# Loads of mem in fewer, longer pieces, and the short convolution behind the other mixers

## The chip, the cores and the metric

The kernel runs on one core of one Trainium2 chip. The metric is the device time of one execution in microseconds (us), the median of several runs. Engines are named as in the profile: PE is TensorE (PEld its weight loads), DVE is VectorE, ACT is ScalarE, POOL is GpSimd, SP is SyncE, which here only issues DMAs.

## The reference

One layer of an encoder for 256 tokens of width 2048, all in float32, with 256 rows of memory for the cross attention:

```python
mem_n = rms_norm(mem, mem_norm_g)
h = rms_norm(x, norm_g[l, 0])
q, k, v, g, lr, u_f, u_h, u_s = jnp.split(h @ w_in[l], split_at, axis=-1)
y_a = gla_mixer(q, k, v, g, lr, ...)                      # gated linear attention
y_b = rms_norm(fnet_mixer(u_f), grp_norm_g[l, 0])         # Fourier mixer
y_c = rms_norm(hyena_mixer(u_h, hy_conv_w[l], filt, hy_skip[l]), grp_norm_g[l, 1])
y_d = rms_norm(shortconv_mixer(u_s, sc_conv_w[l]), grp_norm_g[l, 2])
mix = jnp.concatenate([y_a, y_b, y_c, y_d], axis=-1)
x = x + mix @ w_out[l]
x = x + cross_attention(rms_norm(x, norm_g[l, 1]), mem_n, w_xq[l], w_xkv[l], w_xo[l])
x = x + swiglu(rms_norm(x, norm_g[l, 2]), w_gate_up[l], w_down[l])
return rms_norm(x, final_norm_g)
```

The short convolution mixer is small: `b, c, h = split(u)`, then `b * short_conv(c * h)`, a convolution of three taps along the tokens. Each of the four mixers gives 512 of the 2048 columns of `mix`.

## The kernel before

**Precision and the weight stream.** Each float32 operand of a large product is split in two parts, high and low, and a product is three matmuls: high by high, high by low, low by high (`part_rows`, L345 to L347, for results with tokens on the partitions; `mm`, L296 and L297, for results with features on the partitions). The weights are laid out in HBM in the order of their use, in slabs of 128 x 2048. `Stream._half` loads a slab from SP (L81) into one of three `raw` buffers, and for each half of it (1024 columns) makes the high part on ACT (`wh`, L102) and the low part on DVE (`wl`, L103). `Stream.take` hands the blocks to the products and keeps three halves ahead in this part of the kernel. Activations that enter a product are split likewise into slots of 512 columns, `act[0]` to `act[23]` (act_76 to act_99 in the program): `split`, with the high part from ACT (L206) and the low part from DVE (L198).

**The start.** `w_xkv` comes first, on `mem`. The first slab is loaded in four pieces (256, 256, 512 and 1024 columns), the next ones in halves, as long as the list `st.after` is not empty. After each piece one entry of that list is called; an entry loads parts of `memT` into `res` (`load`, L413), one part being 128 rows of 1 KB (256 columns of float32). Part 0 comes separately (`mem0`). Ten entries load parts 1 to 15: parts 1 to 5 one by one, then pairs. `start_m(n)` scales and splits part n into slot n right before the n-th k-step of the product (L210 on ACT, L202 on DVE).

**The background.** While PE works through the long products, the mixers advance step by step as Python generators in `Background.q`. Behind each matmul group `poll` goes through the list from its front and advances each entry whose time has come, as long as the estimated debt of DVE (`owed`) is small. So an entry nearer to the front has its instructions emitted first when several are due. `drain(g)` advances one generator to its end. Each generator's instructions go into the in-order queues of PE, ACT and DVE between those of the weight stream; a scheduler in the framework then settles the final order on each engine.

**Around the change.** In `mixers`, the Fourier mixer (`fn.mix`) and the gated linear attention (`gl.mix`, GLA) are added at the end of the list; the short convolution (`short_conv`) is added later, at position 0, so ahead of them, and advanced by its first step at once (`go`), which issues the loads of its inputs from POOL. Its further steps are the three-tap convolutions (`conv3`), the products with the first third of `u` (which comes from the last `w_in` product, `ev_s`), and `group_norm`: squares, sums over features on PE (`rstd_begin`, L244), a reciprocal root in small DVE steps (`rstd_cols`, L255 to L258 and helpers), two diagonal matrices `dgh` and `dgl` (`rstd_end`, L273 on ACT and L202 on DVE), a pair of matmuls that spreads the scale over all partitions (L280), a copy of it to `rs` (L283), and the scaled and split result. GLA ends in the same kind of norm, one pair of L280 for each of its four heads; its scaled output is `go`, the gated product `gg`.

**`out_proj`.** The product with `w_out` follows. It takes its sixteen k-steps in four parts in this order: Hyena (slots 16 to 19), Fourier (0 to 3), GLA (4 to 7), short convolution (20 to 23). Ahead of the second, third and fourth part `ready` drains the mixer that the part needs, and then issues loads of rows of `x` into the `res` buffers that this mixer has given up (L714, and L413 for `xT`):

```python
self.mix = act[4:8] + act[0:4] + act[16:24]
return self.gemm_rows("w_out", [0, 512], self.mix, parts=[range(k, k + 4) for k in (8, 4, 0, 12)], before=ready)
```

with `before` being `lambda n: self.bg.drain((g_fn, g_gla, g_sc)[n])`. Each k-step has two column groups and two row groups, twelve matmuls. When the product is done, `add_rows` adds `x` to it.

Of the kernel before, what the change touches and what calls it, by code (L numbers as in the profile page):

```python
# [169 lines left out]
class Block:  # L170
# [219 lines left out]
    def run(self):  # L390
        nc, cp = self.nc, self.cp
        st = self.st
        self.act = [cp.tile([P, 512], F32R, name=f"act{i}") for i in range(24)]
        self.res = [cp.tile([P, 4, R], F32, name=f"res{i}") for i in range(4)]
        self.resk = lambda i: self.res[i // 4][:, i % 4, :]
        self.vec = cp.tile([P, NV], F32, name="vec")
        self.onesr = cp.tile([P, P], F32R, name="ones")
        self.ones = self.onesr.bitcast(F32)
        self.ident = cp.tile([P, P], F32, name="ident")

        self.sq = [cp.tile([P, 8], F32, name=f"sq{i}") for i in range(2)]
        self.mg = cp.tile([P, 16], F32, name="mg")
        self.eps = cp.tile([P, 8], F32, name="eps")[:, 0:1]
        self.gap(cp, 416)

        self.kd = self.outside("keys", KT)
        self.xf = [self.outside(n, KT) for n in ("features1", "features2")]
        self.qf = self.outside("queries", KT)
        self.sf, self.gf, self.gq = (self.outside(n, 4) for n in ("products", "gates", "gla"))
        self.ff = self.outside("hidden", FT)  # L410
        self.vd = nc.dram_tensor("values", (P, 8 * 512), F32, kind="Internal").ap()
        def load(src, k, n):
            nc.sync.dma_start(self.res[k // 4][:, k % 4:k % 4 + n, :].rearrange("p k r -> p (k r)"),  # L413
                              self.t[src][:, k * R:(k + n) * R])

        self.load_x = lambda k, n: load("xT", k, n)

        nc.vector.memset(self.ones, 1.0)

        p = self.bank()  # L420
        for _ in range(10):
            nc.tensor.matmul(p[:, 0:P], self.ones, self.ones, start=True, stop=True)
        nc.vector.memset(self.eps, EPS)
        nc.scalar.copy(self.eps, self.eps)
        st.after = [lambda: None, lambda: None]
        st.after += [lambda a=a: load("memT", *a) for a in ((1, 1), (2, 1), (3, 1), (4, 1), (5, 1), (6, 2), (8, 2), (10, 2), (12, 2), (14, 2))]
        st.after.append(lambda: nc.sync.dma_start(self.vec, self.t["vecs"]))
        make_identity(nc, self.ident)
        with self.tc.tile_pool(name="wx", bufs=1) as st.extra:
            self.attention(self.mixers())  # L430
        self.mlp()
# [5 lines left out]
    def mixers(self):  # L437
# [63 lines left out]
        def short_conv(u0):  # L501

            m = []
            for k in range(4):
                m.append(self.tmp())
                self.load_turned(m[-1], self.sf, k)
            yield FAR
            for j in range(4):
                m[j] = self.conv3(m[j], V_SCW + 3 * j)
                yield  # L510
            sq = []
            for j in range(4):
                while len(u0) <= j:
                    yield
                y = self.res[1][:, j, :]
                self.tt(y, y, m[j], ALU.mult)
                sq.append(self.tmp())
                nc.scalar.activation(sq[j], y, AF.Square)
                if j > 1:
                    self.tt(sq[j - 1], sq[j - 2], sq[j - 1], ALU.add)  # L520
                yield SOON
            yield from self.group_norm(self.res[1], 2, act[20:24], total=sq[2:])

        with tc.tile_pool(name="mid", bufs=1) as mid:
            self.dgp = mid
            gl = Gla(self, mid)
            with tc.tile_pool(name="hyp", bufs=1) as hyp, tc.tile_pool(name="k2", bufs=8) as k2:
                hy = Hyena(self, hyp, k2)

                mem0 = hy.piece()[:, 0:R + 16]  # L530
                nc.sync.dma_start(mem0, self.t["mem0"])
                self.bg.add(prepare(mid))

                for cols in ([0, 512], [1024], [1536]):
                    first = dict(parts=[[k] for k in range(KT)], before=start_m) if len(cols) > 1 else {}
                    for c, ps in zip(cols, self.gemm_rows("w_xkv", cols, h, **first)):
                        for r in range(2):
                            self.store_turned(self.kd, c // P, r, hy.piece(), ps[r][:, :])
                for hd in range(4):
                    for r, p in enumerate(self.gemm_rows("w_xkv", [D + hd * 512], h, start_x if hd == 3 else rows.append)[0]):  # L540
                        for c in range(2):
                            v, o = self.tmp(), (2 * hd + r) * 512 + c * R
                            nc.scalar.activation(v, p[:, c * R:(c + 1) * R], AF.Copy, scale=self.rcm[:, r:r + 1])
                            nc.gpsimd.dma_start(self.vd[:, o:o + R], v)
                    if hd < 2:
                        self.load_x(8 * hd, 4)
                        self.load_x(8 * hd + 4, 4)
                self.bg.drain()

                def ev_u(i, p):  # L550
                    hy.feed(i, self.merge(p))
                    if i == 4:
                        self.bg.add(hy.convs())

                self.gemm("w_in", [UH + i * P for i in range(12)], h, ev_u)
                for r, p in enumerate(self.gemm_rows("w_in", [512], h, lambda k: k or low_rank())[0]):
                    nc.scalar.copy(gl.v[r], p)
                for r, p in enumerate(self.gemm_rows("w_in", [0], h)[0]):
                    for j in range(0, 512, R):
                        self.store_turned(self.gq, j // P, r, self.tmp(), p[:, j:j + R])  # L560
                gl.fetch()
                fn = Fnet(self, act[20:24])
                fn.feed(self.gemm_rows("w_in", [UF], h)[0])
                self.bg.drain()

            with tc.tile_pool(name="glp", bufs=1) as glp:
                gl.open(glp)
                fn.open(glp)
                g_fn = self.bg.add(fn.mix(act[0:4], gl))
                g_gla = self.bg.add(gl.mix(act[4:8]))  # L570
                halves = [(r, j) for r in range(2) for j in range(0, 512, R)]
                ps = self.gemm_rows("w_in", [US + 512], h)[0]
                c = [self.tmp() for _ in halves]
                for t, (r, j) in zip(c, halves):
                    nc.scalar.copy(t, ps[r][:, j:j + R])
                ps = self.gemm_rows("w_in", [US + 1024], h)[0]
                for t, (r, j) in zip(c, halves):
                    self.tt(t, ps[r][:, j:j + R], t, ALU.mult)
                    self.store_turned(self.sf, j // P, r, self.tmp(), t)
                u0 = []  # L580
                g_sc = self.bg.add(short_conv(u0), 0, True)
                ps = self.gemm_rows("w_in", [1024], h)[0]
                for r, j in halves:
                    t = self.tmp()
                    nc.scalar.activation(t, ps[r][:, j:j + R], AF.Silu)
                    self.store_turned(self.gf, j // P, r, self.tmp(), t)
                for k in range(4):
                    self.load_turned(gl.gate[k], self.gf, k)

                def ev_s(i, p):  # L590
                    u0.append(i)
                    self.merge(p, self.res[1][:, i, :])

                self.gemm("w_in", [US + i * P for i in range(4)], h, ev_s)
                gl.done = True
                return self.out_proj(lambda n: self.bg.drain((g_fn, g_gla, g_sc)[n]))
# [429 lines left out]
class Hyena:  # L1026
# [100 lines left out]
    def load(self):  # L1127

        nc, t = self.b.nc, self.b.t
        nc.sync.dma_start(self.tab, t["dft"][:, 512:1024])  # L1130
        fwd = self.piece()
        nc.sync.dma_start(fwd, t["dft"][:, 0:512])
        small = self.piece()
        c33, w2 = small[0:33, 0:R + 64], small[0:64, R + 64:R + 128]
        nc.sync.dma_start(c33, t["c33"])
        nc.sync.dma_start(w2, t["c64"][0:64, 0:64])
        self.loaded = fwd, c33, w2
        self.decay(0)
# [508 lines left out]
```

## Time and profile before

| | us |
|---|---|
| median of 3 runs | 1478.79 (1477.31 to 1478.9) |
| profiled execution, own time | 1480.23 |
| its span | 1478.4 |
| PE busy | 1464.6 (99%) |
| DVE busy | 930.4 (63%) |
| ACT busy | 745.7 (50%) |
| POOL busy | 179.7 (12%) |

The mean granted clock of TensorE was 0.996 of full speed. How to read the lines that follow: a row of a timeline gives start, duration, engine, source line, operation and tiles (output, arrow, inputs), and in square brackets the idle time before it and what ended that. A row of waits names who waited for whom, the sum, how often, and the longest. A row of windows gives, for a stretch, the busy time of PE, PEld, DVE, ACT and POOL, then the granted clock (1.00 is full speed), the busy share of the DMA engines and the GB/s that they moved. A group of DMA issues gives its count, its size and the median time from issue to landing. Starts of matmuls are exact, their ends are modelled, so the distance between starts is the better measure.

### The profile page before, as it was taken

How to read it: one execution, taken by the hardware profiler on the slowest of the kernel's cores; microseconds unless marked ns; L12 is line 12 of the kernel's file. 1: busy time of each engine (PE TensorE's matmuls, PEld its weight loads, DVE VectorE, ACT ScalarE, POOL GpSimd, SP SyncE). 2: the span in 40 equal slices, each digit the busy share in tenths (PEclk: the TensorE clock that was granted, in tenths of full speed). 3: DMA queues.
4: the chain of work that ended last, by engine and by line, in shares of the span. 5: the costliest groups of instructions: out<-in, count | busy, mean ns of one | idle time of the engine just before them, and what ended most of it. 6: DMA issues, size and time to landing. Idle time of an engine off the chain costs nothing.

```text
span 1478.4 us, 18218 instructions
## 1 busy us (share of the span) xinstructions
PE 1464.6 (99%) x6832; PEld 1219.3 (82%) x6832; DVE 930.4 (63%) x1336; ACT 745.7 (50%) x1079; POOL 179.7 (12%) x240
## 2 busy tenths in 40 slices
PE   9999999999999999999999999999999999999997
PEld 7888888888888788888888888888888888888886
DVE  6677868777776676886765554555555456544444
ACT  6566655446655464665554444444444445434344
POOL 0000100021020323420501100111110111000000
PEclk9999999999999999999999999999999999999999
DMA  9786654465665687764856666666666666555554
GB/s 351 280 286 241 216 193 165 156 205 190 202 194 193 198 256 239 239 204 151 254 194 215 220 210 218 215 217 224 226 209 204 218 221 229 186 191 195 199 197 145
DMA packets 58328, 315.97 MB, mean 214 GB/s; under 512 B 8925, under 2 KB 10622, under 8 KB 26624
## 3 DMA queue, kind: packets, MB, share of 16 engines
q1 hardware_dynamic: 46064, 281.11, 55.9%
q0 software_dynamic: 11744, 33.04, 8.5%
q8 instruction: 53, 0.87, 0.2%
q10 hardware_dynamic: 432, 0.66, 0.1%
q14 instruction: 35, 0.29, 0.1%
HBM read 296.43 MB, written 18.35 MB: 213 GB/s over the span
## 4 chain that ended last, share of the span: by engine, by line
PE 96%; ACT 1%; DVE 1%; DMA 1%; issue 0%; SPq 0%; ACTq 0%
PE pg L345 26%; PE pg L346 25%; PE pg L347 25%; PE pg L296 7%; PE pg L297 4%; PE pm L346 1%; PE pm L345 1%; PE pm L347 1%; PE pm L1106 1%; PE pm L874 1%; PE pm L846 0%; DMA raw<-in_W 0%; ACT wh L102 0%; DVE wl L103 0%; DMA tmp<-in_cfn 0%
## 5 line engine op out<-in xcount | busy, mean ns | idle before, releaser
L103 DVE TENSOR_TENSOR wl<-raw,wh 128x1024 fp32r<-128x1024 f32 (+1 forms) x503 | 611.3, 1217 | 473.1 <-ACT wh L102 471.8
L102 ACT CAST wh<-raw 128x1024 fp32r<-128x1024 f32 (+1 forms) x503 | 523.6, 1043 | 583.3 <-PE pg L347 505.3
L345 PE MATMUL pg<-wh,act 128*128 128x512 f32 (+1 forms) x1562 | 611.4, 392 | 1.9 <-ACT wh L102 1.1
L346 PE MATMUL pg<-wl,act 128*128 128x512 f32 (+1 forms) x1562 | 609.1, 390 | 0.8 <-DVE wl L103 0.8
L347 PE MATMUL pg<-wh,act 128*128 128x512 f32 (+1 forms) x1562 | 609.1, 390 | 0.0
L345 PEld LDWEIGHTS pg<-wh,act 128*128 128x128 f32 x1562 | 294.2, 188 | 65.5 <-ACT wh L102 1.5
L346 PEld LDWEIGHTS pg<-wl,act 128*128 128x128 f32 x1562 | 294.1, 188 | 61.8 <-DVE wl L103 2.2
L347 PEld LDWEIGHTS pg<-wh,act 128*128 128x128 f32 x1562 | 294.0, 188 | 61.5
L296 PE MATMUL pg<-act,wh 128*128 128x512 f32 x432 | 152.0, 394 | 0.0
L297 PE MATMUL pg<-act,wl 128*128 128x256 f32 x432 | 121.0, 280 | 0.0
L296 PEld LDWEIGHTS pg<-act,wh 128*128 128x128 f32 x432 | 81.2, 188 | 17.4
L297 PEld LDWEIGHTS pg<-act,wl 128*128 128x128 f32 x432 | 81.2, 188 | 0.3
L382 POOL DMA_DIRECT2D hidden<-u x22 | 16.7, 763 | 408.3 <-DVE u L380 408.3
L345 PE MATMUL pg<-wh,f 128*128 128x512 f32 x120 | 46.7, 389 | 0.0
L346 PE MATMUL pg<-wl,f 128*128 128x512 f32 x120 | 46.7, 389 | 0.0
L347 PE MATMUL pg<-wh,f 128*128 128x512 f32 x120 | 46.7, 389 | 0.0
L387 POOL DMA_DIRECT2D tmp<-hidden x44 | 38.9, 890 | 41.5 <-ACT wh L102 20.5
L345 PEld LDWEIGHTS pg<-wh,f 128*128 128x128 f32 x120 | 22.5, 188 | 4.7
L347 PEld LDWEIGHTS pg<-wh,f 128*128 128x128 f32 x120 | 22.5, 188 | 4.7
L346 PEld LDWEIGHTS pg<-wl,f 128*128 128x128 f32 x120 | 22.5, 188 | 4.6
L382 POOL DMA_DIRECT2D features<-tmp x24 | 17.1, 717 | 73.6 <-DVE tmp L380 73.6
L387 POOL DMA_DIRECT2D mr<-keys x16 | 14.2, 889 | 55.7 <-DVE act L198 48.9
(314 smaller groups left out, 1136.1 us busy)
## 6 DMA issues: line engine op xcount, KB each, us to landing
raw<-in_W SPq DMA_DIRECT2D x246, 1024.0 KB, 5.0
raw<-in_W SPq DMA_DIRECT2D x11, 512.0 KB, 7.2
hidden<-u POOLq DMA_DIRECT2D x22, 256.0 KB, 3.5
tmp<-hidden POOLq DMA_DIRECT2D x44, 128.0 KB, 4.6
features<-tmp POOLq DMA_DIRECT2D x24, 128.0 KB, 2.3
res<-in_xT SPq DMA_DIRECT2D x5, 512.0 KB, 6.6
ar<-features POOLq DMA_DIRECT2D x20, 128.0 KB, 6.2
k<-in_mem SPq DMA_DIRECT2D x8, 256.0 KB, 6.7
```

Source lines behind the costliest of these rows:

```text
L102: nc.scalar.copy(wh[:, a:b], r[:, a:b])
L103: nc.vector.tensor_tensor(out=wl[:, a:b], in0=r[:, a:b], in1=wh[:, a:b].bitcast(F32), op=ALU.subtract)
L296: self.nc.tensor.matmul(p[:, :], wh, slot[:, :], start=start, stop=False)
L297: self.nc.tensor.matmul(p[:, 0:R], wl, slot[:, 0:R], start=False, stop=stop)
L345: self.nc.tensor.matmul(p, hi, wh, start=start, stop=False)
L346: self.nc.tensor.matmul(p, hi, wl, start=False, stop=False)
L347: self.nc.tensor.matmul(p, lo, wh, start=False, stop=stop)
L382: self.nc.gpsimd.dma_start(to[r], u.rearrange("p (k c) -> p k c", c=P))
L387: self.nc.gpsimd.dma_start(t.rearrange("p (g t) -> p g t", t=32), src)
L874: nc.tensor.matmul(p[:, :], vh[m][:, s], pt[m][:, :], start=m == 0, stop=False)
L1106: self.b.nc.tensor.matmul(p, a, b, start=start and n == 0, stop=stop and n == 2)
```

## The change

Two lines change. The first edit replaces the list of loads of `memT`: parts 1 and 2 come as one load, then 3, then 4 and 5, 6 and 7, 8 to 11, and 12 to 15: six loads in place of ten, with rows of 1, 2 or 4 KB. Four entries of the list are now empty, so that the pieces of the slabs keep their number and sizes. The second edit adds the short convolution at the end of the background's list instead of its front.

```diff
         st.after = [lambda: None, lambda: None]
-        st.after += [lambda a=a: load("memT", *a) for a in ((1, 1), (2, 1), (3, 1), (4, 1), (5, 1), (6, 2), (8, 2), (10, 2), (12, 2), (14, 2))]
+        st.after += [lambda a=a: a and load("memT", *a) for a in ((1, 2), (), (3, 1), (4, 2), (), (6, 2), (8, 4), (), (12, 4), ())]
         st.after.append(lambda: nc.sync.dma_start(self.vec, self.t["vecs"]))
...
                 u0 = []
-                g_sc = self.bg.add(short_conv(u0), 0, True)
+                g_sc = self.bg.add(short_conv(u0), go=True)
                 ps = self.gemm_rows("w_in", [1024], h)[0]
```

In the program that comes of it, PE, DVE and ACT carry the same instructions in another order, POOL the same in the same order; SP has four DMAs fewer. Each engine's order differs in two stretches: the first k-steps of `w_xkv`, and the stretch from the last `w_in` products to the end of `out_proj`.

## The prediction

> **What bounds the kernel now.** I read the page first, then what PE waited for, then the clock by stretch, then the timelines of PE and DVE around the one long wait.
>
> ```profile
> span 1478.4 us, 18218 instructions
> PE 1464.6 (99%) x6832; PEld 1219.3 (82%) x6832; DVE 930.4 (63%) x1336; ACT 745.7 (50%) x1079; POOL 179.7 (12%) x240
> ```
>
> TensorE is the bound all along: 13.8 us of the span are not PE. So a change can gain only where PE waits or where its matmuls run slower than elsewhere. The waits of PE:
>
> ```profile
> PE pm L280 <- DVE dgl L202: 2.2, 2, 1.8
> PE pg L345 <- ACT wh L102: 1.1, 1, 1.1
> ...
> PE pg L345 <- ACT act L206: 0.8, 1, 0.8
> PE pg L346 <- DVE wl L103: 0.8, 3, 0.4
> ```
>
> The first and third lie together, in `out_proj`; the second is the start. The granted clock in `out_proj`:
>
> ```profile
> 478.00:482.20 4.20, 1.19 (x5) 0.60 (x4) 3.89 (x12) 2.63 (x6) 0.00 (x0) 0.81 0.35 117
> 482.20:487.60 5.40, 5.40 (x13) 4.23 (x14) 3.63 (x9) 1.22 (x3) 1.16 (x2) 0.51 0.27 61
> ```
>
> In the first stretch PE is busy 1.19 of 4.20 us; in the second it is fully busy, at half clock (0.51). So the wait is paid twice, and the second payment is in no list of waits. Its size, from PE's timeline:
>
> ```profile
> 473.39 0.28 PE L280 MATMUL pm<-dgh,ones 128*128 128x256 f32 x1
> ...
> 473.62 0.39 PE L345 MATMUL pg<-wh,act 128*128 128x512 f32 x1
> ...
> 475.06 0.39 PE L345 MATMUL pg<-wh,act 128*128 128x512 f32 x1
> ...
> 477.56 0.39 PE L347 MATMUL pg<-wh,act 128*128 128x512 f32 x1
> 477.79 0.31 PE L280 MATMUL pm<-dgh,ones 128*128 128x256 f32 x1
> 479.89 0.38 PE L280 MATMUL pm<-dgl,ones 128*128 128x256 f32 x1 [1.79 <-DVE dgl L202]
> ...
> 482.18 0.79 PE L345 MATMUL pg<-wh,act 128*128 128x512 f32 x1 [0.82 <-ACT act L206]
> 482.77 0.63 PE L346 MATMUL pg<-wl,act 128*128 128x512 f32 x1
> ...
> 487.04 0.59 PE L347 MATMUL pg<-wh,act 128*128 128x512 f32 x1
> ...
> 488.18 0.40 PE L345 MATMUL pg<-wh,act 128*128 128x512 f32 x1
> ```
>
> At full clock, weight matmuls start 0.227 us apart (475.06 to 477.56, eleven steps) and an L280 takes 0.115 (473.39 to 473.62, two). From 477.79 to 488.18, 10.39 us, PE starts four L280 and fifteen weight matmuls, worth 4 x 0.115 + 15 x 0.227 = 3.87. **Lost: 6.5 us**: 3.9 before 482.18 (4.39 less 0.46), the other 2.6 at the low clock.
>
> Why PE waits there: the four L280 spread the norm scales of the last two GLA heads, and need `dgl` from DVE. DVE's order:
>
> ```profile
> 474.14 0.65 DVE L202 SCALAR_TENSOR_TENSOR dgl<-ident,rc,dgh 128x128 fp32r<-128x128 f32 x2 [0.24 <-ACT dgh L273]
> 474.70 1.27 DVE L202 SCALAR_TENSOR_TENSOR res<-res,vec,rs 128x256 f32<-128x256 f32 x3
> 475.89 1.22 DVE L103 TENSOR_TENSOR wl<-raw,wh 128x1024 fp32r<-128x1024 f32 x1
> 477.02 0.88 DVE L202 SCALAR_TENSOR_TENSOR go<-go,vec,rs 128x256 f32<-128x256 f32 x2
> ...
> 479.22 0.61 DVE L202 SCALAR_TENSOR_TENSOR dgl<-ident,rc,dgh 128x128 fp32r<-128x128 f32 x2
> ...
> 480.12 0.61 DVE L202 SCALAR_TENSOR_TENSOR dgl<-ident,rc,dgh 128x128 fp32r<-128x128 f32 x2
> ```
>
> The `res` rows are the short convolution's norm, done ahead of GLA's `dgl` although `out_proj` needs the short convolution last (slots 20 to 23, after GLA's 4 to 7).
>
> **Second edit, the short convolution last in line.** Nothing is added or removed: the same instructions stand in another order on PE, ACT and DVE; POOL's order is unchanged. Call the sixteen k-steps of `out_proj` halves 0 to 15 (12 matmuls, 2.73 us each): Hyena 0 to 3, Fourier 4 to 7, GLA 8 to 11, short convolution 12 to 15. In the changed program's order, GLA's first two L280 pairs stand in half 1 and its last two in half 3 (before: between halves 6 and 7, and just ahead of half 8); the short convolution's sums (L244) stand between halves 5 and 6, its one L280 pair in the middle of half 10. Walked with these rows:
>
> ```profile
> 454.01 0.40 PE L345 MATMUL pg<-wh,act 128*128 128x512 f32 x1
> ...
> 462.28 0.95 PE L244 MATMUL pm<-ones,tmp 128*128 128x1 f32 x8
> 463.09 0.48 PE L345 MATMUL pg<-wh,act 128*128 128x512 f32 x1
> ```
> ```profile
> 463.26 0.16 DVE L255 TENSOR_SCALAR rc<-pm 128x2 f32<-128x2 f32 x1 [1.14 <-PE pm L244]
> 463.46 0.17 DVE L257 TENSOR_SCALAR rc<-rc 128x2 uint32<-128x2 uint32 x1
> ```
> ```profile
> 480.36 0.37 ACT L283 COPY rs<-pm 128x256 f32<-128x256 f32 x1 [0.62 <-PE pm L280]
> ...
> 481.72 0.41 ACT L206 CAST act<-gg 128x256 fp32r<-128x256 f32 x1
> ```
>
> Half 0 starts at 454.01 as before, as the same PE work lies ahead of it. GLA's last pairs come at 454.01 + 3 x 2.73 + 0.46 + 9 x 0.227 = 464.7. Behind them ACT has two copies (0.37), a weight cast (taken as long as its split, 1.22) and four casts (0.41); DVE two `go` steps (0.88), two products, a weight split (1.22) and four subtractions, each taken like a cast. That is 5 to 6 us, so slots 4 to 7 are ready near 470. Half 8 starts at 454.01 + 8 x 2.73 + 8 x 0.115 + 0.81 (L244) = 477.6: **margin 7 us**, and the wait is gone, with the low clock behind it.
>
> What is late next is the short convolution. Its L244 ends at 472.2; the reciprocal root is 14 small DVE steps 0.20 apart, 2.8 us, with two weight splits between, then `dgh` and `dgl` (0.61 a pair, `dgh` taken alike), 1.2: ready at 478.5 with the weight work between, for a PE pair at 484.4 (half 10 at 483.0, six matmuls on). Margin 6. From that pair to slot 20: second L280 until 484.9, copy 0.37, three `res` steps 1.27 (the cast lies beside them), a subtraction taken as 0.41: ready at 487.0. Half 12 starts at 477.6 + 4 x 2.73 + 0.23 = 488.7. **Margin 1.7 us**, the thinnest place; the cast and split of half 14 stand behind slot 20, so slots 21 to 23 come near 489 to 490, for halves from 491.5 on.
>
> SP: the x rows for `res[1]` move behind two more weight loads, as they must wait until slot 23 has been read:
>
> ```profile
> 478.60 0.33 SPq L714 DMA_DIRECT2D res<-in_x  x1
> ```
> ```profile
> res<-in_x SPq DMA_DIRECT2D x4, 256.0 KB, 2.9
> ```
> ```profile
> 507.13 1.25 DVE L198 TENSOR_TENSOR res<-res,pg 128x512 f32<-128x512 f32 x2
> ```
>
> Issued at 490 instead of 478.6, landed 3 to 6 us later, used at about 507.1 - 6.5 = 500.6: hidden, costs nothing; without that cover it would cost its lateness. The weight load behind it waits for half 15's split, near 491, so it is not held. The load of `res[3]` moves forward past one weight load; it waits for GLA's sums, which now end earlier: nothing. I take -6.5; ends: -3.9 (the clock falls anyway, somewhere else) and -6.9 (from 454.01 to 477.79 PE took 23.8 us, by the walk's terms, with six L280, 23.3: small stops that may go too).
>
> [...]
>
> **First edit, the loads of mem.** Ten loads become six; bytes stay.
>
> ```profile
> 3.08 0.43 SPq L413 DMA_DIRECT2D res<-in_memT  x1
> ...
> 3.55 0.56 SPq L81 DMA_DIRECT2D raw<-in_W  x1
> ```
> ```profile
> 6.20:9.00 2.80, 2.58 (x16) 2.03 (x15) 1.09 (x2) 1.03 (x2) 0.00 (x0) 1.00 1.00 305
> 9.00:10.50 1.50, 0.41 (x3) 0.05 (x1) 0.07 (x1) 0.72 (x2) 0.00 (x0) 1.00 0.95 296
> ```
> ```profile
> 10.45 0.51 PE L345 MATMUL pg<-wh,act 128*128 128x512 f32 x1 [1.09 <-ACT wh L102]
> ...
> 11.18 0.50 PE L346 MATMUL pg<-wl,act 128*128 128x512 f32 x1 [0.22 <-DVE wl L103]
> ```
>
> PE's second wait ends with the fourth piece of the first slab (the wait at 10.45). Part 2 of mem now goes ahead of that piece: 128 KB more, at 305 GB/s 0.43 us later at most. Against this: the slot of 0.47 us (3.08 to 3.55) ahead of slab 1 goes, so slab 1 may come that much earlier; and PE's order now puts two L345 ahead of the first L346, which fills 0.23 of the 0.5 us between 10.45 and 11.18 that is not matmul, though the same pairing is lost at slab 1. Ends -0.3 (slab 1 is 0.47 earlier, less a part of the lost pairing) and +0.45; I take +0.1, near the middle, as gain and loss come from rows of like size. Later mem loads have PE work of many microseconds ahead of them.
>
> [...]
>
> **Sum.** -6.5 + 0.1 = -6.4 on the profiled execution's own 1480.23 (span 1478.4 and 1.8 around it) is 1473.8; it was 1.4 above the median of the runs, 1478.79, from which the forecast goes: **1472.4**.
>
> **The rivals.**
> - *The short convolution becomes the wait, and the kernel is slower.* Its place: L280 of half 10 to slot 20. For: it is the thinnest margin, and the chain crosses PE, ACT and DVE five times. Against: the weight cast ahead of it (half 13's, free to start when half 9 ends at 483.0) is done by 484.3 in the walk, ahead of the pair's copy. PE idles for what the chain is late beyond 1.7 us; once it idles 4 us the clock costs 2.6 more. To lose the 6.4 it must come 6 us later than walked; at 9 us late, 1482. Chance 5%.
> - *Part of the wait comes back there.* 2 us of idling, without the clock 1474.4, with it 1477.0. Chance 8%.
> - *The gain is given back behind `out_proj`*, because weights or x rows then arrive late: about 1478.8. Against: in these stretches DMA moved 61 to 117 GB/s, against 305 at the start. Chance 4%.
> - *The start's gap grows and the clock falls there*: 0.45 + 2.6 on top, 1475.4. Against: PE's 1.09 us of idling left the clock at 1.00 in 9.00:10.50, and 1.5 is well under the 4.2 that halved it. Chance 4%.
>
> **How the numbers follow.** Forecast 79%, own range 1470.8 to 1473.5: ends -6.9 - 0.3 and -6.5 + 0.45 on 1478.79, with 0.8 to each side for the runs (1477.31 to 1478.9). The range given, 1470.8 to 1475.2, takes in the milder return; left out are its clocked half, the given-back, the start's and the slower case, 17%. Within 0.2% (3 us, about what a measurement here can tell) lies the given-back case and a little of the return: 5%. Slower 5%, faster 90%.
>
> **What would show it.** Right: no wait of PE on L280 `dgl` or on `act` L206 in 470 to 490, clock 1.00 throughout `out_proj`, half 12 starting near 489, PE's busy time down by about 2.6. The first edit: the L345 at 10.45 within 0.45 us of that. Wrong: a wait of L345 on `act` at half 12, a clock under 1.00 anywhere between 10 and 1460 us, or PE waiting for `wl` or `raw` after 490.

## The result, and the profile after

The changed kernel took 1473.82 us in the median of 7 runs (1473.27 to 1474.22), the kernel before 1478.73 (7 runs, 1477.31 to 1479.65): a ratio of 0.9967, 95% interval 0.9956 to 0.9978. The change makes the kernel faster by 4.9 us; the interval allows 3.3 to 6.5. The forecast was 1472.4, in a range of 1470.8 to 1475.2.

The profiled execution took 1474.11 us. Its page begins:

```profile
span 1472.3 us, 18220 instructions
PE 1461.3 (99%) x6832; PEld 1217.1 (83%) x6832; DVE 929.6 (63%) x1336; ACT 745.5 (51%) x1079; POOL 179.4 (12%) x240
```

PE's waits after the change (waiting engine, tile and line, arrow, who ended it; then sum, how often, longest):

```profile
PE pg L345 <- ACT wh L102: 1.2, 2, 0.9
PE pm L422 <- DVE eps L423: 1.1, 1, 1.1
PE pg L346 <- DVE wl L103: 0.4, 2, 0.2
PE pg L345 <- DVE res L198: 0.3, 1, 0.3
```

The waits on `dgl` (L280) and on `act` (L206) of before are gone. The start's wait on `wh` is still there, and the last line is new. The two stretches of `out_proj` that the prediction showed, and the rest of the kernel behind them:

```profile
478.00:482.20 4.20, 4.20 (x20) 3.50 (x19) 1.74 (x4) 2.10 (x2) 0.00 (x0) 1.00 0.56 176
482.20:487.60 5.40, 5.40 (x26) 4.46 (x26) 3.89 (x7) 2.65 (x4) 0.00 (x0) 1.00 0.56 193
492.00:1460.00 968.00, 967.97 (x4402) 805.43 (x4402) 560.08 (x731) 459.77 (x624) 131.57 (x165) 1.00 0.65 212
```

PE is busy throughout at a granted clock of 1.00. In the first stretch it starts 20 matmuls instead of 5, in the second 26 instead of 13. From PE's timeline after the change, the sums and pairs of the two norms, the new wait, and the start of half 12:

```profile
456.40 0.39 PE L345 MATMUL pg<-wh,act 128*128 128x512 f32 x1
457.08 0.51 PE L345 MATMUL pg<-wh,act 128*128 128x512 f32 x1 [0.28 <-DVE res L198]
457.42 0.40 PE L346 MATMUL pg<-wl,act 128*128 128x512 f32 x1
...
465.34 0.28 PE L280 MATMUL pm<-dgl,ones 128*128 128x256 f32 x1
471.60 0.95 PE L244 MATMUL pm<-ones,tmp 128*128 128x1 f32 x8
484.75 0.28 PE L280 MATMUL pm<-dgh,ones 128*128 128x256 f32 x1
...
489.11 0.39 PE L345 MATMUL pg<-wh,act 128*128 128x512 f32 x1
```

GLA's last pair comes at 465.3, the short convolution's pair at 484.8, and neither is waited for. In half 1 PE stops: two steps of 0.227 take 1.02 us (456.40 to 457.42), 0.57 lost. DVE's rows behind the short convolution's pair, and ACT's first cast of slot 20:

```profile
485.86 1.27 DVE L202 SCALAR_TENSOR_TENSOR res<-res,vec,rs 128x256 f32<-128x256 f32 x3
487.05 0.42 DVE L198 TENSOR_TENSOR act<-res,act 128x256 fp32r<-128x256 f32 x1
```
```profile
486.37 0.41 ACT L206 CAST act<-res 128x256 fp32r<-128x256 f32 x1 [0.81 <-DVE res L202]
```

The high part of slot 20 is ready at 486.8, its low part at 487.5.

How much of the difference lies in `out_proj`, in the same 38 us of both profiles. Before:

```profile
454.00:492.00 38.00, 34.99 (x148) 28.11 (x147) 26.06 (x62) 19.45 (x36) 4.06 (x5) 0.91 0.62 192
```

After:

```profile
454.00:492.00 38.00, 37.72 (x175) 31.16 (x174) 29.73 (x61) 20.52 (x36) 4.06 (x5) 1.00 0.68 218
```

PE starts 27 more matmuls, 27 x 0.227 = 6.1 us. That is the whole of the difference between the two spans (1478.4 to 1472.3). So between these two executions the sum of 6.4 was 0.3 too large; between the medians it was 1.5 too large. The experiments look for the rest.

### The profile page after: what moved, and what is told of

It is laid out like the page before. It is cut to its first block, busy times and chain, and to the rows that moved or that the text cites. A ratio compares the mean times of both kernels' runs of the same rounds, so it can differ in the third digit from the quotient of the medians.

```text
span 1472.3 us, 18220 instructions
## 1 busy us (share of the span) xinstructions
PE 1461.3 (99%) x6832; PEld 1217.1 (83%) x6832; DVE 929.6 (63%) x1336; ACT 745.5 (51%) x1079; POOL 179.4 (12%) x240
## 4 chain that ended last, share of the span: by engine, by line
PE 96%; ACT 1%; DVE 1%; DMA 1%; issue 0%; SPq 0%; ACTq 0%
PE pg L345 26%; PE pg L346 26%; PE pg L347 25%; PE pg L296 7%; PE pg L297 3%; PE pm L347 1%; PE pm L345 1%; PE pm L346 1%; PE pm L1106 1%; PE pm L874 1%; PE pm L846 1%; DMA raw<-in_W 0%; DVE wl L103 0%; DMA tmp<-in_cfn 0%; ACT wh L102 0%
## 5 line engine op out<-in xcount | busy, mean ns | idle before, releaser
L345 PE MATMUL pg<-wh,act 128*128 128x512 f32 (+1 forms) x1562 | 611.2, 391 | 1.4 <-ACT wh L102 1.2
L345 PEld LDWEIGHTS pg<-wh,act 128*128 128x128 f32 x1562 | 293.4, 188 | 64.4 <-ACT wh L102 1.8
L345 PE MATMUL pg<-wh,f 128*128 128x512 f32 x120 | 46.7, 389 | 0.0
L345 PEld LDWEIGHTS pg<-wh,f 128*128 128x128 f32 x120 | 22.5, 188 | 4.6
L901 ACT ACTIVATE g<-pg,rc 128x512 f32<-128x512 f32 x22 | 15.0, 689 | 9.6 <-PE pg L347 9.6
```

The costliest lines, as they stand in the source:

```text
L345: self.nc.tensor.matmul(p, hi, wh, start=start, stop=False)
L901: nc.scalar.activation(g[r], ps[r], AF.Silu, scale=box["col"][:, r:r + 1])
```

## The experiments

### The two edits apart

The second edit alone:

```diff
-                g_sc = self.bg.add(short_conv(u0), 0, True)
+                g_sc = self.bg.add(short_conv(u0), go=True)
```

> The second edit alone. Theory (the whole gain is the wait in out_proj and the low clock behind it): 1473.6 to 1474.2, as with both edits, no wait of PE on L280, clock 1.00 throughout out_proj. Rival (the first edit gives a share of the gain): 1475 or more.

Measured: 1472.70 us (5 runs, 1472.56 to 1472.82), ratio 0.9962 [0.9949, 0.9976]. The second edit alone carries the whole gain; the time is 0.9 us below the range that was expected.

The first edit alone:

```diff
-        st.after += [lambda a=a: load("memT", *a) for a in ((1, 1), (2, 1), (3, 1), (4, 1), (5, 1), (6, 2), (8, 2), (10, 2), (12, 2), (14, 2))]
+        st.after += [lambda a=a: a and load("memT", *a) for a in ((1, 2), (), (3, 1), (4, 2), (), (6, 2), (8, 4), (), (12, 4), ())]
```

> The first edit alone. Theory: within 0.5 us of the kernel before, 1478.3 to 1478.9, with the wait on L280 and the half clock still there; PE 0.2 us earlier at 17 us, as in the trace with both edits. Rival (the first edit gives a share): 1477.5 or less.

Measured: 1479.44 us (11 runs, 1478.22 to 1480.33), ratio 1.0004 [0.9995, 1.0013]. By the 95% interval a gain of more than 0.7 us is excluded, and a loss of more than 1.9. The median lies 0.5 us above the range that was expected.

The kernel before once more, with no edit, as a measure of the measurement:

> The kernel before, unchanged, to see the low clock in other executions. Theory A (the wait of 3.9 us is the same each time, the length of the stretch at half clock is not, and the execution in the profile before had a long one): the spans differ by up to 2 us and the mean clock differs with them, 0.996 for the long ones and 0.997 for the short ones; the profile here shows the same 3.9 us of waiting and a clock share of 1.0 to 2.6 us. Rival B (the low clock is the same each time, and the missing 1.4 us lie elsewhere): a clock share of 2.6 us again, with a span that is shorter in another place.

Measured: 1478.76 us (11 runs, 1477.32 to 1479.67), ratio 1.0002 [0.9994, 1.0011]. The profiled execution took 1478.80. Its waits on `dgl` and `act` are those of before (2.2 and 0.8 us in sum); its low clock is shown below.

The medians put both edits together 1.1 us above the second edit alone. Whether that is the first edit's cost is taken up below.

### What the low clock is worth

The stall stays; PE gets dummy products in it, so that it is not idle (15 matmuls of 512 columns into a bank that nobody reads: 8 and 2 behind the `dgh` matmuls of the two last heads, 5 behind the last `dgl`; they are extra work and change no result).

```diff
+            q = self.bank() if warm else None
...
+                for _ in range(warm if d is dg[0] else tail):
+                    nc.tensor.matmul(q[:, :], self.onesr, self.act[16], start=True, stop=True)
...
-            rest = [b.rstd_end(col, h + i) for i in range(2)]
+            rest = [b.rstd_end(col, h + i, None, *((8, 0), (2, 5))[i] if h else ()) for i in range(2)]
```

> The kernel before, with fifteen extra matmuls of 512 columns put where PE waits in out_proj: eight between the first L280 of the pair before half 8 and its second, two in the next pair, five after it. They compute nothing that is used. The wait stays, the idling goes, so this measures the clock's share alone. Theory A: clock 1.00 in out_proj, the wait still ends near 482.2, time 1477.0 to 1477.6 (the median before less a clock share of 1.2 to 1.7), and the executions lie within 1 us of each other, as they do after the change. Rival B (the clock's share is always 2.6): 1476.2. Rival C (PE at work does not keep the clock up): 1478.7 or more.

Measured: 1476.52 us (11 runs, 1475.78 to 1477.34), ratio 0.9987 [0.9978, 0.9995]. The same 38 us:

```profile
454.00:492.00 38.00, 38.00 (x173) 30.56 (x172) 27.51 (x62) 19.41 (x36) 4.05 (x5) 1.00 0.60 187
```

The clock stays at 1.00 although PE does no more useful work during the stall: 173 less the 15 dummies are 158 of the kernel's own matmuls. The product goes on 1.38 us behind the last `dgl` matmul of the stall (1.40 before), so the dummies do not hold it up. So the low clock is a cost by itself: 2.0 to 2.2 us by the medians (1478.52 for before beside it, 1478.76 for before run again, less 1476.52), 1.9 by the ratio with an interval of 0.7 to 3.3. That lies between the two figures that were expected, 1.2 to 1.7 and 2.6, and excludes neither. In this profile before's 148 matmuls are 10 fewer, 2.3 us.

Why is it not always the same? The first edit alone has the same stall, but its profile shows the low clock for half as long. Rows of one microsecond at the edges; where the clock falls from 1 to one half within a row, the share of the row at half rate is twice what is missing to 1. Before:

```profile
480.00:481.00 1.00, 0.60 (x3) 0.40 (x3) 0.96 (x4) 0.37 (x1) 0.00 (x0) 0.82 0.46 148
481.00:487.00 6.00, 5.18 (x12) 3.86 (x13) 4.56 (x11) 1.90 (x5) 0.56 (x1) 0.50 0.27 65
487.00:488.00 1.00, 1.00 (x5) 0.76 (x4) 0.00 (x0) 0.33 (x1) 1.00 (x2) 0.77 0.82 262
```

Before, run again (in the six rows between the two the clock is 0.50):

```profile
478.00:479.00 1.00, 0.50 (x2) 0.30 (x2) 1.00 (x5) 0.38 (x2) 0.00 (x0) 0.97 0.59 178
...
485.00:486.00 1.00, 1.00 (x4) 0.77 (x4) 0.00 (x0) 0.00 (x0) 1.00 (x2) 0.62 1.05 172
...
454.00:492.00 38.00, 35.00 (x148) 28.12 (x147) 26.45 (x61) 18.55 (x36) 4.06 (x5) 0.91 0.61 185
```

The first edit alone:

```profile
480.00:481.00 1.00, 0.13 (x1) 0.13 (x1) 0.92 (x4) 0.77 (x2) 0.00 (x0) 0.68 0.58 203
481.00:483.00 2.00, 2.00 (x5) 1.61 (x6) 2.00 (x7) 1.16 (x3) 0.00 (x0) 0.50 0.09 30
483.00:484.00 1.00, 1.00 (x4) 0.77 (x4) 1.00 (x1) 0.06 (x1) 0.00 (x0) 0.62 0.00 0
...
454.00:492.00 38.00, 34.90 (x153) 28.28 (x152) 26.89 (x62) 19.55 (x37) 4.05 (x5) 0.96 0.61 187
```

Before: 0.36 + 6 + 0.46 = 6.82 us at half rate. Before, run again: 0.06 + 6 + 0.76 = 6.82 as well, and again 148 matmuls. So between these two executions the low clock is the same and the 1.4 us lie elsewhere, as rival B had it; where, the section on the start shows. The first edit alone: 0.64 + 2 + 0.76 = 3.40, just half of it, and five more matmuls done in the 38 us, 1.1 us.

The stall is the same in the three, but the clock falls at another point of it: 2.9 us behind the first `dgh` matmul of the stall in before (477.79 to 480.64), 2.6 in before run again (476.37 to 478.94), 3.8 in the first edit alone (476.60 to 480.36). So the same stall was followed by 6.82 us at half rate in two profiles and by 3.40 in one; what decides between the two lengths, three profiles don't show.

How often before has the longer stretch, no trace counts. The mean granted clock of an execution, which is known for every run, gives a hint: it is 0.996 in both profiles of before and 0.997 in that of the first edit alone. Of the 27 executions of before beside these runs, 16 have 0.997 and take 1478.04 us in the mean, 10 have 0.996 and take 1479.21. The distance, 1.17 us, is about the 1.1 between the two lengths. The mean also takes in the end of the span, where the clock is low too (0.50 from 1474 to 1478 in before, with PE idle), so it is a hint and no more.

### Must the short convolution stand behind GLA?

Both edits, but the short convolution second in line, behind the Fourier mixer and ahead of GLA:

```diff
-                g_sc = self.bg.add(short_conv(u0), go=True)
+                g_sc = self.bg.add(short_conv(u0), 1, True)
```

> Both edits, but the short convolution put at position 1 of the line, behind the Fourier mixer and ahead of GLA. Theory (what counts is that its norm stands ahead of GLA's dgl): the wait on L280 just before half 8 comes back in part, the clock falls behind it, 1476 to 1479. Rival (being behind the Fourier mixer is enough): 1473.5 to 1474.3.

Measured: 1473.19 us (4 runs, 1472.02 to 1475.17), ratio 0.9963 [0.9948, 0.9977]. PE has no wait on L280 or `act` at this place in line either. From PE's timeline:

```profile
466.56 0.95 PE L244 MATMUL pm<-ones,tmp 128*128 128x1 f32 x8
...
472.57 0.28 PE L280 MATMUL pm<-dgl,ones 128*128 128x256 f32 x1
481.56 0.28 PE L280 MATMUL pm<-dgh,ones 128*128 128x256 f32 x1
```

GLA's last pair comes 7.2 us later than with both edits (465.34), the short convolution's pair 3.2 earlier (484.75), and PE waits for neither. So it was enough to take the short convolution from the head of the line. But this run doesn't test what its theory names. DVE's order in it:

```profile
463.88 1.14 DVE L202 SCALAR_TENSOR_TENSOR dgl<-ident,rc,dgh 128x128 fp32r<-128x128 f32 x4
...
467.54 0.16 DVE L255 TENSOR_SCALAR rc<-pm 128x2 f32<-128x2 f32 x1 [0.38 <-PE pm L244]
...
472.98 0.35 DVE L202 SCALAR_TENSOR_TENSOR dgl<-ident,rc,dgh 128x128 fp32r<-128x128 f32 x1 [0.24 <-ACT dgh L273]
```

The four `dgl` steps of the last two heads stand ahead of the short convolution's reciprocal root and of its own `dgl`, although the short convolution is ahead of GLA in the list. With both edits it is so too (462.82, 472.59 and 477.69); before it was the other way round. So the theory's condition, the norm ahead of GLA's `dgl`, was not met here, and the prediction's account of the wait ("ahead of GLA's `dgl`") fits all three kernels. What falls is only that the short convolution has to be last in the list.

### How thin is the thinnest margin?

Both edits, and the scale `rs` of the short convolution's norm passes through 9, then 18 more steps on DVE in series (each leaves it as it is), so that slot 20 comes late:

```diff
+        for _ in range(late):
+            self.nc.vector.scalar_tensor_tensor(out=rs, in0=rs, scalar=1.0, in1=rs, op0=ALU.mult, op1=ALU.max)
```

> Both edits, and nine more DVE steps of about 0.43 us in a row on the spread scale of the short convolution's norm (each multiplies by one and keeps the value), so slot 20 is 3.9 us later, and 2.3 more for two weight splits that now stand ahead. Measured after the change, slot 20 was ready 2.1 us ahead of its need. Theory (the rival of the prediction, with its price): PE waits about 4.1 us at half 12 and the clock falls, 1479 to 1481. Without a fall of the clock: 1477.9. If the margin was larger than read: less than 1476.

> The same with eighteen steps: slot 20 is 10.0 us later. Theory (the wait is paid in full, the clock's share does not grow with it): a wait of 7.9 us, 1483 to 1485. Rival (the clock's share grows with the idling): 1486 or more.

Measured: with 9 steps 1479.75 us (10 runs, 1478.38 to 1481.02), ratio 1.0007 [0.9998, 1.0016]; with 18 steps 1483.79 (7 runs, 1482.56 to 1485.98), ratio 1.0033 [1.0021, 1.0044]. From the timelines with 9 steps (PE's, then DVE's):

```profile
483.30 0.28 PE L280 MATMUL pm<-dgh,ones 128*128 128x256 f32 x1
...
491.54 0.50 PE L345 MATMUL pg<-wh,act 128*128 128x512 f32 x1 [3.72 <-ACT act L206]
```
```profile
484.40 2.26 DVE L624 SCALAR_TENSOR_TENSOR rs<-rs 128x256 f32<-128x256 f32 x5
...
490.56 1.27 DVE L202 SCALAR_TENSOR_TENSOR res<-res,vec,rs 128x256 f32<-128x256 f32 x3
```

And with 18:

```profile
484.88 0.28 PE L280 MATMUL pm<-dgh,ones 128*128 128x256 f32 x1
...
497.26 0.79 PE L345 MATMUL pg<-wh,act 128*128 128x512 f32 x1 [7.86 <-ACT act L206]
```

In the changed kernel the `res` steps follow the pair by 1.11 us (484.75 to 485.86) and half 12 by 4.36 (484.75 to 489.11). With 9 steps the `res` steps follow by 7.26, so they are 6.15 late, more than 9 steps, as two weight splits (1.22 us each, from 486.58 and 489.43) now get ahead of them; half 12 follows by 8.24, 3.88 late. **The margin is 6.15 less 3.88, 2.3 us.** That is the margin of slot 20's high part, for which PE waits here (`act` L206), and it is what the changed kernel's rows say: ready at 486.8, needed at 489.1. The prediction's 1.7 was reckoned to the low part, which comes last; the rows give 1.6 for it (487.5 to 489.1). The chain that was 6.15 us late took the whole gain, as the rival's price had it ("6 us later"). With 9 steps the low clock lasted 0.20 + 3 + 0.20 = 3.40 us (0.90 in 492 to 493, 0.50 in the three rows behind it, 0.90 in 496 to 497). The low clock with 18 steps:

```profile
491.00:492.00 1.00, 0.00 (x0) 0.00 (x0) 1.00 (x2) 0.00 (x0) 0.00 (x0) 0.72 0.00 0
492.00:501.00 9.00, 3.74 (x9) 2.93 (x10) 7.08 (x18) 1.60 (x4) 0.00 (x0) 0.50 0.46 149
501.00:502.00 1.00, 1.00 (x5) 0.77 (x4) 0.00 (x0) 0.00 (x0) 0.00 (x0) 0.66 0.56 191
```

0.56 + 9 + 0.68 = 10.24 us, three times 3.41 (half of before's 6.82). But PE works in it only from 497.26 to 501.68, 4.4 us; the rest is the wait itself. So the longer stall cost its length and still only 2.2 us of clock behind it; its time fits the theory (1483 to 1485), not the rival.

### Does the start pay for the first edit?

Both edits, with the last piece of the first slab cut in two, so that its first half may land earlier:

```diff
-CUTS = {0: [0, 256, 512, 1024, 2048]}
+CUTS = {0: [0, 256, 512, 1024, 1536, 2048]}
```

> Both edits, and the last piece of the first slab (1024 columns) cut in two of 512. Theory (PE's wait at 10.5 us ends with the landing of that piece, so a smaller one ends it sooner): that wait 0.3 to 0.9 us shorter, 1473.0 to 1473.6. Rival (the DMA queue is the limit, the half piece lands hardly sooner and the extra issue costs): 1473.6 to 1474.3.

Measured: 1474.03 us (5 runs, 1472.85 to 1474.35), ratio 0.9964 [0.9951, 0.9977]: no difference from both edits. In its profile PE doesn't wait for `wh` at the start, but neither does it in a second profile of both edits below, so whether the cut piece helps stays open.

Then four kernels together on one chip: both edits again, the second edit alone again, the short convolution second in line with the old loads, and both edits with part 1 alone ahead of the fourth piece. The diffs of the last two, against before and against both edits:

```diff
-                g_sc = self.bg.add(short_conv(u0), 0, True)
+                g_sc = self.bg.add(short_conv(u0), 1, True)
```
```diff
-        st.after += [lambda a=a: a and load("memT", *a) for a in ((1, 2), (), (3, 1), (4, 2), (), (6, 2), (8, 4), (), (12, 4), ())]
+        st.after += [lambda a=a: a and load("memT", *a) for a in ((1, 1), (2, 2), (), (4, 2), (), (6, 2), (8, 4), (), (12, 4), ())]
```

> Both edits once more, unchanged, beside the second edit alone on one chip. Theory A (the first edit costs about 1 us, because the load of parts 1 and 2 stands ahead of the fourth piece of the first slab, and because of the new wait of 0.45 us in the second half of out_proj): 1473.5 to 1474.2, 0.9 to 1.4 above the second edit alone. Theory B (the start only varies from one execution to the next, and the five runs of the second edit alone were lucky ones; only the wait in out_proj is the first edit's): 0.2 to 0.5 above it.

> The second edit alone once more. Theory A: 1472.4 to 1472.9, few runs above 1473.2. Theory B: median near 1473.2, with runs up to 1474, as the start comes late in it as often as in the others.

> The old loads of mem, and the short convolution between the Fourier mixer and GLA. No wait of PE in out_proj is expected by either theory. Theory A: 0.9 us under both edits, 1472.3 to 1472.9, at or just under the second edit alone, as the halves of out_proj had no wait at this place in line. Theory B: 1472.5 to 1473.3, the same as with the new loads at this place (1473.19).

> Both edits, but part 1 of mem is loaded alone ahead of the fourth piece, as before, and parts 2 and 3 together behind that piece; the other loads are the first edit's. Theory A with the place of part 2 as its cause: near the second edit alone, 1472.4 to 1473.1, with the wait in out_proj perhaps left (0.45). Theory A with another cause, in the later and longer loads: as both edits, 1473.5 to 1474.2. Theory B: all within 0.5 us of each other.

| | median, us | runs | ratio, 95% interval |
|---|---|---|---|
| both edits | 1473.25 | 1472.71 to 1474.01 (5) | 0.9964 [0.9952, 0.9977] |
| second edit alone | 1473.25 | 1472.22 to 1473.45 (5) | 0.9961 [0.9947, 0.9974] |
| second in line, old loads | 1473.99 | 1471.87 to 1475.17 (5) | 0.9967 [0.9955, 0.9980] |
| part 1 alone | 1473.32 | 1472.52 to 1473.96 (5) | 0.9964 [0.9951, 0.9976] |

Theory A falls: no step of 1 us between the first two, and none that follows the loads. Theory B stands in the main, though its 0.2 to 0.5 between the first two didn't show, and the third kernel came out above what either theory had for it, with the widest spread (1471.87 to 1475.17).

What varies is the start, from execution to execution of the same kernel. PE's first 20 us in the profile of before, and in that of the same kernel run again:

```profile
0.00:20.00 20.00, 17.39 (x77) 14.37 (x78) 11.06 (x20) 12.45 (x21) 0.71 (x6) 1.00 0.88 306
```
```profile
0.00:20.00 20.00, 18.31 (x83) 14.81 (x84) 12.36 (x22) 13.65 (x23) 0.70 (x6) 1.00 0.89 315
```

77 matmuls started in the one and 83 in the other, 6 x 0.227 = 1.4 us, and the two executions took 1480.23 and 1478.80 us. In the second, PE did not wait for `wh` at the start at all. The stall in `out_proj` and its low clock were the same in both. In the other profiles the longest such wait was between none and 1.3 us, with old and new loads alike. The longest was in the kernel with the old loads and the short convolution second in line. Its waits of PE, and then its clock by stretches:

```profile
PE pg L345 <- ACT wh L102: 1.7, 2, 1.3
```
```profile
10.00:11.00 1.00, 0.30 (x1) 0.19 (x1) 0.33 (x1) 0.97 (x2) 0.00 (x0) 0.94 1.00 392
11.00:14.00 3.00, 2.94 (x7) 2.10 (x7) 2.53 (x5) 2.66 (x5) 0.00 (x0) 0.50 1.04 409
14.00:15.00 1.00, 1.00 (x5) 0.77 (x5) 1.00 (x3) 0.83 (x2) 0.00 (x0) 0.86 1.04 410
```

Here the clock fell behind it, for 0.12 + 3 + 0.28 = 3.40 us; that execution took 1475.11, and this kernel's fastest 1471.87.

One thing does go with both edits together: the new wait in half 1 on `res` (L198), 0.57 us lost. It is in all five profiles with the new loads and the short convolution last (both edits twice, six pieces, and the 9 and 18 steps), and in the one with part 1 alone. It is in neither profile of the second edit alone, and not with the short convolution second in line. In the waits of PE of both edits again, and in PE's timeline of the second edit alone (1472.70), at the same place:

```profile
PE pg L345 <- DVE res L198: 0.3, 1, 0.3
```
```profile
455.73 0.81 PE L345 MATMUL pg<-wh,act 128*128 128x512 f32 x2
456.38 0.39 PE L346 MATMUL pg<-wl,act 128*128 128x512 f32 x1
```

Two steps take 0.65 us there, 0.2 lost instead of 0.57. DVE's rows show where the difference begins, 7 us earlier. A weight split (the first row is from the changed kernel, the second from the second edit alone):

```profile
449.68 1.23 DVE L103 TENSOR_TENSOR wl<-raw,wh 128x1024 fp32r<-128x1024 f32 x1 [0.27 <-ACT tmp L303]
```
```profile
448.65 1.22 DVE L103 TENSOR_TENSOR wl<-raw,wh 128x1024 fp32r<-128x1024 f32 x1
```

In the first the split starts 0.43 us behind the start of the small step before it (449.25), held until an ACT copy (L303) is done; in the second 0.08 behind it (448.57). The 0.35 stays in DVE's chain up to the `res` step, and PE loses about that much more (0.57 less 0.2). Four of the profiles with the new wait (the changed kernel, six pieces, 9 and 18 steps) have this hold of 0.27 on L303 in DVE's rows; those of the second edit alone (1472.70) and of the short convolution second in line (1473.19) don't. Over all runs, on several chips, both edits have a median of 1473.70 (12 runs) and the second edit alone 1472.74 (10). About 0.4 of the difference is this wait; that the rest is chance is likely by the run on one chip, but not shown. Why loads at the start bring in a hold 440 us later isn't known. No version was shown to beat both edits; the second edit alone is at least as fast.

## Why the prediction was right, and where it was wrong

**The bound and the cause: right.** The stall in `out_proj` was paid twice, as wait and as low clock. With the short convolution behind the others both are gone, and the second edit alone carries the gain. The clock's part was shown by itself: dummy products without any earlier data gave 1.9 to 2.2 us. The signs that the prediction named came: no wait on L280 or on `act`, clock 1.00 throughout `out_proj`, no low clock up to 1460 us. PE's busy time fell by 3.3 us (1464.6 to 1461.3) where 2.6 was expected; the ends of matmuls are modelled, so this is not read further.

**The range: partly luck.** 1473.82 lies in the range given, 1470.8 to 1475.2, but above the forecast's own, 1470.8 to 1473.5. The part above 1473.5 had been added for a milder return of the wait at the short convolution, and that wait did not come. In the second series both edits had 1473.25, inside the forecast's own range.

**The walk: right.** Half 12 began at 489.11 (predicted 488.7), slot 20 was ready at 487.5 (487.0), the short convolution's pair came at 484.75 (484.4), GLA's last pairs at 464.99 to 465.34 (464.7). The margin from the low part of slot 20 to half 12 was 1.6 us (1.7). The x rows for `res[1]` were issued at 489.37 (about 490) and cost nothing: no wait stands behind 490 in PE's list. What the walk lacked was a stop: it took half 1 as 2.73 us, and there the new wait on `res` takes 0.57. Half 12 is only 0.4 us late all the same because in this execution `out_proj` began 0.35 us earlier than walked (453.66).

**The term that was mis-sized: "the other 2.6 at the low clock"**, and with it the 6.5 as a figure for the median. For the profile that it was read from it is right. The second edit alone, in the same 38 us:

```profile
454.00:492.00 38.00, 38.00 (x177) 31.49 (x176) 28.68 (x58) 20.84 (x37) 4.06 (x5) 1.00 0.69 215
```

PE starts 177 matmuls against 148 before, 29 x 0.227 = 6.6 us, and before run again has 148 too. In both the low clock lasted 6.82 us. But the same stall doesn't always bring that much: in the profile of the first edit alone it brought 3.40, with five more matmuls, 1.1 us: then 5.5 are lost. The clock's share as measured over eleven runs, 1.9 to 2.2, lies between the two cases, as if the executions of before were a mixture; the mean clocks hint at that, no trace counts it. By this share the sum should have had about 6.0 for the stall, less the 0.57 in half 1: 5.4, where 4.9 was measured with an interval of 3.3 to 6.5. With 3.40 us at half rate, as in the first edit alone, the clock's share would be 1.7 in place of 2.6 and the sum 1473.3 (an estimate from that profile), nearer to 1473.82. The profile of before had 6.82, which by the mean clocks not every execution seems to have.

**The first edit: +0.1, in its range of -0.3 to +0.45 as far as can be told.** Alone it measured +0.6 us by its ratio, with an interval of -0.7 to +1.9; on one chip the second edit with and without it had the same median. The wait at 10.45 moved to 10.53 in the profile after, but that says little: in another execution of before the same wait was not there at all. Together with the second edit the new loads do cost something, but in a place at which the term didn't look: the wait in half 1, 0.57 us instead of 0.2.

**The rivals.** The short convolution as the next wait: its price was right where it was made late (6.15 us late, gain gone; 1483.8 with 18 steps, later than the 9 us for which the prediction had 1482). It didn't happen, as the margin held. The start's clock: it can happen, and the argument against it was wrong. The prediction held it off as "1.5 is well under the 4.2 that halved it"; in one profile the clock fell to 0.50 at a start whose longest wait was 1.28 us. That execution took 1475.11, where the rival had 1475.4. It happened with the old loads, so it doesn't need the new ones.

**The step to the median.** The profiled execution of before was 1.4 us above the median. Against before run again, at 1478.80, that is the start: six matmuls fewer in the first 20 us, and the same stall. As the start varies alike in both kernels, leaving the 1.4 out was sound; what was not is that the clock's share of one profile went into the median whole.

## What to carry to other kernels

Where several background chains feed one product, put them in line in the order in which the product needs them: a chain that is needed last and worked first delayed the one that was needed earlier, and moving it cost nothing as long as its own margin held. Where the granted clock falls at a stall of the bound engine, as here, count the stall as its length and a clock term, and take that term from several executions, not from a single trace: here the same stall came with 3.40 us at half rate in one profile and 6.82 in two. Before a small term is read from one profile, run the same kernel twice: here the start alone moved by 1.4 us.

## What the runs showed of the hardware

- The low clock inside the kernel lasted 3.40 us in three profiles (the first edit alone, 9 steps, the start of the old loads with the short convolution second), 6.82 in two (before, twice), 10.24 in one (18 steps): about once, twice and three times 3.41.
- The clock fell also behind waits shorter than those of the stall in `out_proj`. At the start of the profile with the old loads and the short convolution second it fell at 10.88, when PE had waited 0.43 us up to 7.24, 0.23 up to 7.97 and 1.28 up to 10.70; in another profile (the second edit alone, again) waits of 0.28 us up to 7.14, 0.22 up to 7.86 and 1.11 up to 10.40 left it at 1.00. What separates the two isn't shown.
- PE's start on the fourth piece of the first slab moved by more than a microsecond between executions of one program, with old and new loads alike: its first L345 on that piece came at 10.45 and 9.02 in the two profiles of before, at 10.53 and 9.43 in the two of both edits. In the first three ACT's cast of that piece, which the load's landing released, began at 9.78, 8.32 and 9.86.
